# Two-layer hybrid trunk on one Trainium2 core: activation rows split with an adding transfer, wide products one group sooner, runs of three in both layers

## Chip, core and metric

The kernel runs on one core of a Trainium2 chip. The metric is the time of one execution of the whole program on the device in microseconds (us), as the median of several runs. The engines are named as the profile names them: PE is TensorE, which multiplies matrices (PEld is its loading of weights), DVE is VectorE, ACT is ScalarE, POOL is GpSimd, SP is SyncE. SP issues the loads from memory; POOL issues the transfers that add while they copy. All of them are carried by the core's 16 DMA engines.

## The reference

The input is x with 512 tokens of 1024 numbers. Two layers run one after the other. Each has a mixer (layer 0: short convolution and pooling heads; layer 1: spatial gating in chunks) and then a gated feed-forward block with a causal convolution between up-projection and activation. The change is in the feed-forward block of both layers:

```python
def gated_conv_ffn(x, w_gate, w_up, conv_w, conv_b, w_down):   # D_FF = 2816
    g = jnp.einsum('bsd,df->bsf', x, w_gate)
    g = causal_dwconv3(g, conv_w) + conv_b
    up = jnp.einsum('bsd,df->bsf', x, w_up)
    return jnp.einsum('bsf,fd->bsd', jax.nn.silu(g) * up, w_down)
...
        hn = rms_norm(h, norm_ffn[layer])
        h = h + gated_conv_ffn(hn, w_ffn_gate[layer], w_ffn_up[layer], conv_ffn[layer],
                               b_conv_ffn[layer], w_ffn_down[layer])
    return rms_norm(h, final_norm)
```

All numbers are 32-bit floats.

## The kernel before

**Numbers in two parts.** Every operand of a matmul is kept as a high part, rounded to the reduced format that TensorE takes (float32r), and a low part, what the rounding left. A product is three matmuls: high by high, high by low, low by high. To split a tile, `halves` and `split` (L262) let ScalarE write the high part (L265) and VectorE subtract it from the source (L267). The other way, `summed` (L137), lets ScalarE write the negated, rounded source into the low part (L141), lets a transfer issued by POOL add the source to it (L143), and lets ScalarE write the high part after that (L145). Both give the same two parts, since the low part is the source less its rounding.

**The feed-forward block.** Its 2816 columns are 22 tiles of 128, taken two at a time: f = 0, 2, ..., 20. f=0 is multiplied directly. Every other group of two tiles is computed with the Strassen-Winograd form of a 2 x 2 block product: seven products for the gate `g` and seven for the up-projection `u`, fourteen in the order of `todo` in `products`. Each has four row blocks of 128 (kp = 0 to 3), and each row block takes three matmuls of 256 columns (line 705 of `multiply`). A *wide* product joins two of the three: the high part of the weights multiplies the high and the low part of the moving operand side by side, in one matmul of 512 columns, and the low part of the weights follows with one of 256 (line 695). The two halves of the bank then have to be added: where a narrow product is folded with one VectorE add, or one ScalarE copy (L944), a wide one takes one more VectorE add of 256 columns (L932). For `u`'s product 4 this is a copy and an add (L981 and after it).

**Which are wide.** `FIRST_WIDE` gives, for each layer, the first f at which all products of `g` and of `u` are wide; at the first f of `g`, products 2, 5 and 3 of `u` are too. So the first wide group has ten wide products of fourteen, and the later ones fourteen.

**Their order.** `parts_of` lists, for each product, whether the 512-column matmuls or the 256-column ones (`True` in `lows`) come first. Where all are wide, layer 0 alternates: the first product wide then narrow, the second narrow then wide, and so on. Layer 1 puts three products' narrow matmuls in a row and then three products' wide ones.

**What feeds a group.** `prepare(f)` loads four raw weight tiles of 512 KB on SP's queue, forms the sums that the scheme needs (s12, s34) on VectorE and splits them. The second raw tile of `g` and of `u` goes the way of `summed` (wlo_g, wlo_u); from f=4 on so do s12 and s34 of `g` (L887 to L889). A raw buffer is free for the next load when the last reader, the adding transfer among them, is done.

**The rows.** After a group, VectorE and ScalarE convolve, apply silu and multiply by `u`; this gives two activation rows of 128 x 512. `act` (L752) splits a row with `split` into a_hi and a_lo, for which there are four buffers each. `STEPS` sets when a down-projection runs: two groups' rows (four) are multiplied with one half of the output's columns after the next group and with the other half after the one behind that. The rows of the next two groups can be split only as that second half frees the four buffers. Layer 0's last four rows are used by `d_last`; layer 1's last four are not split by `act` but in the block that ends the kernel.

**What sets the order.** The kernel is written for a framework that orders the instructions of each engine when it is built: among those that are ready by its own costs, the one that stands earlier in the program goes first. `behind` adds an order by hand between two instructions of an engine, `inorder` keeps a stretch as it is written. On the chip each engine, POOL's issues among them, then runs its list in that order, and each instruction waits for its semaphores.

Of the kernel before, what the change touches and what calls it, by code (L numbers as in the profile page):

```python
# [9 lines left out]
F32R = mybir.dt.float32r  # L10
BF16 = mybir.dt.bfloat16
AF = mybir.ActivationFunctionType
ALU = mybir.AluOpType
PSUM = bass.MemoryType.PSUM

P = 128
D = 1024
S = 512
# [3 lines left out]
NF = FF // P  # L22
# [9 lines left out]
def tile_trunk(ctx: ExitStack, tc: tile.TileContext, x, norm_mix, norm_ffn, final_norm,  # L32
# [3 lines left out]
    nc = tc.nc  # L36
# [44 lines left out]
    def behind(ins, first):  # L81

        if first is not None:
            tc.add_manual_dep(ins.ins, first.ins.name, mybir.DependencyInfo(
                mybir.DependencyClass.NoSync, mybir.DependencyReason.DATA), reason="order")
# [176 lines left out]
    def split(pool, src, name, scale=1.0, tag="a", bufs=None):  # L262
        hi = pool.tile([P, S], F32R, tag=f"{tag}hi", bufs=bufs, name=f"{name}_hi")
        lo = pool.tile([P, S], F32R, tag=f"{tag}lo", bufs=bufs, name=f"{name}_lo")
        nc.scalar.activation(hi, src, AF.Copy, scale=scale)  # L265
        if isinstance(scale, float):
            nc.vector.tensor_tensor(lo, src, hi.bitcast(F32), ALU.subtract)  # L267
        else:
            nc.vector.scalar_tensor_tensor(lo, src, scale, hi.bitcast(F32),
                                           op0=ALU.mult, op1=ALU.subtract)  # L270
        return hi, lo
# [15 lines left out]
    def padded_tile():  # L287
        turn[0] += 1
        return padded[turn[0] % NPADDED]
# [382 lines left out]
    PAIRS = [k for i in range(NP) for k in (i, i + NP)]  # L672

    FIRST_BY_DMA = 4
    FIRST_WIDE = ({"g": 6, "u": 8}, {"g": 4, "u": 6})

    BANK = {1: "a", 6: "a", 7: "a", 4: "a", 5: "e", 3: "e", 2: "b"}

# [37 lines left out]
    class Ffn:  # L716
# [33 lines left out]
            return s  # L750

        def act(self, ft, s):  # L752
            self.acts[ft] = split(self.ap, s, f"a{self.layer}_{ft}", tag="a", bufs=4)

        def pair_weights(self, order):

# [155 lines left out]
        def products(self, f, stat):  # L912

            layer, ap, n = self.layer, self.ap, f"{self.layer}_{f}"
            banks = {"g": {}, "u": {}}
            kept = ap.tile([P, 3, HALF], F32, tag="kept", bufs=1, name=f"kept{n}")
            pads = [padded_tile() for _ in range(2)]
            lo, hi = slice(2, 2 + HALF), slice(2 + HALF, 2 + S)
            dst = {("g", 1): pads[0][:, lo], ("g", 6): pads[0][:, hi], ("g", 7): pads[1][:, hi],
                   ("g", 4): pads[1][:, lo]}  # L920
            dst.update({("u", product): kept[:, i, :] for i, product in enumerate((1, 6, 7))})
            onto = {2: 1, 7: 7, 3: 6}
            s = {}

            def in_both(key, product):
                first = FIRST_WIDE[layer]
                return f >= first[key] or f == first["g"] and product in (2, 5, 3)

            def add(d, bank, halves):
                ins = None  # L930
                for half in halves:
                    ins = nc.vector.tensor_tensor(d, bank[:, half * HALF : (half + 1) * HALF], d,  # L932
                                                  ALU.add)
                return ins

            def after(key, product, bank):
                halves = range(1 + in_both(key, product))
                if product in onto:
                    ins = add(dst[key, onto[product]], bank, halves)
                    if product == 7:  # L940
                        self.added[key] = ins
                elif (key, product) != ("u", 4):
                    d = dst[key, 7 if product == 5 else product]
                    nc.scalar.copy(d, bank[:, :HALF])  # L944
                    add(d, bank, halves[1:])

            todo = [("g", 1), ("u", 1), ("g", 2), ("g", 5), ("g", 6), ("u", 5), ("u", 6),
                    ("g", 7), ("u", 2), ("u", 7), ("g", 3), ("u", 3), ("g", 4), ("u", 4)]
            if layer and all(in_both(*at) for at in todo):
                parts_of = [(0, (False,))]  # L950
                for i in range(0, len(todo), 3):
                    parts_of += [(j, (True,)) for j in range(i, min(i + 3, len(todo)))]
                    parts_of += [(j, (False,)) for j in range(i + 1, min(i + 4, len(todo)))]
            else:
                parts_of = [(i, (i % 2 == 1, i % 2 == 0)) for i in range(len(todo))]
            begun = set()
            for i, lows in parts_of:
                key, product = todo[i]
                bank = self.multiply(banks[key], f"{key}{n}", product, stat[key, product],
                                     in_both(key, product), lows)  # L960
                if len(lows) == 1 and i not in begun:
                    begun.add(i)
                    continue
                after(key, product, bank)
                if (key, product) in (("g", 4), ("g", 3)):
                    j = product == 4
                    row = pads[j][:, 2:]
                    nc.vector.tensor_tensor(row, row, self.r, ALU.mult)  # L968
                    s[j] = self.silu(self.conv(pads[j], f + j), f + j)
                    if j and layer == 0:  # L970
                        nc.vector.tensor_tensor(s[1], s[1], self.r, ALU.mult)
            if layer == 0:
                nc.vector.tensor_tensor(kept[:, :2, :], kept[:, :2, :],
                                        self.r.rearrange("p (a b) -> p a b", a=2), ALU.mult)
            s0 = s[0].rearrange("p (a b) -> p a b", a=2)
            nc.vector.tensor_tensor(s0, kept[:, :2, :], s0, ALU.mult)
            nc.vector.tensor_tensor(s[1][:, HALF:], kept[:, 2, :], s[1][:, HALF:], ALU.mult)
            last = bank[:, :HALF]
            if in_both("u", 4):
                last = kept[:, 0, :]  # L980
                nc.scalar.copy(last, bank[:, :HALF])  # L981
                add(last, bank, (1,))
            nc.vector.tensor_tensor(s[1][:, :HALF], last, s[1][:, :HALF], ALU.mult)
            return [(f + 1, s[1]), (f, s[0])]
# [358 lines left out]
    def ffn1(norm):  # L1343
        with tc.tile_pool(name="f1", bufs=1) as ap:
# [108 lines left out]
            def product(p, i, c0=0, c1=512, bank=None):  # L1453
# [14 lines left out]
                return ps  # L1468

            vec, act, pool = nc.vector, nc.scalar, nc.gpsimd  # L1470
            rows_f = [wp.tile([P, D], F32, tag="raw", bufs=4, name=f"yf{t}") for t in range(NT)]
            factor, root = ([ssf[:, t, i : i + 1] for t in range(NT)] for i in (4, 5))
# [91 lines left out]
            refined(0, 1)  # L1564
            taken(7, 1, right)
            scaled(act, 0, left)
            scaled(act, 0, right)
            stored(0, slice(0, D))
            all_but_last(2, right)
# [84 lines left out]
```

## Time and profile before

| | us |
|---|---|
| median of 3 runs (lowest, highest) | 966.72 (966.33, 968.95) |
| the profiled execution, its own time | 966.66 |
| its span, first to last instruction | 964.9 |

| engine | busy us | share of the span |
|---|---|---|
| PE | 956.6 | 99% |
| DVE | 847.2 | 88% |
| ACT | 620.8 | 64% |
| POOL | 162.4 | 17% |

The granted clock of TensorE is 0.999 over the span. The feed-forward block of layer 0 stands at about 144 to 460 us of the span, that of layer 1 at about 632 us to the end. In the page's row of the 16 DMA engines' busy share, most slices of these stretches stand at 4 to 8 tenths.

How to read the rows that follow: a group row gives line, engine, operation, out<-in by the program's names (without buffer numbers), partitions x elements and count, then busy time in us and the mean duration in ns, then the idle time of the engine before these instructions and who ended it. A row of the timeline starts with the start and the duration in us; what stands in brackets is the idle time before it. Matmuls overlap, so the distance between two starts, and not a matmul's duration, is what TensorE pays for one.

### The profile page before, as it was taken

The page shows a single profiled execution, that of the slowest core. Times are in us where ns is not written, and L with a number is a line of the kernel's source. Part 1 is how long each engine was busy: PE and PEld are TensorE (multiplying, and loading weights), DVE is VectorE, ACT ScalarE, POOL GpSimd, SP SyncE. Part 2 cuts the span into 40 slices and gives each one's busy share as a digit, 9 for nine tenths or more (in the row PEclk, how much of TensorE's full clock was granted, in tenths as well). Part 3 has the DMA queues.
Part 4 walks back from the last instruction along what each step waited for, and adds up shares of the span by engine and source line. Part 5 has one row for each costly group of instructions (what it writes and reads, how often), then busy time and mean ns, then how long its engine had stood idle before and what let it go on. Part 6 is the DMA issues. An engine that isn't in the chain of part 4 may idle for free.

```text
span 964.9 us, 14240 instructions
## 1 busy us (share of the span) xinstructions
PE 956.6 (99%) x5155; PEld 826.5 (86%) x5155; DVE 847.2 (88%) x1435; ACT 620.8 (64%) x944; POOL 162.4 (17%) x183
## 2 busy tenths in 40 slices
PE   9999999999999999999999999999999999999997
PEld 7888898998888888888888888989888888888885
DVE  6887988989899998998878689889998989989898
ACT  5524667766576565765487847787765566646676
POOL 2142333111011010110311002321111011110124
PEclk9999999999999999999999999999999999999999
DMA  7442345777777578774452323467776777667865
GB/s 253 146 141 87 66 144 120 179 188 178 176 174 176 153 175 197 164 180 137 131 153 88 109 88 88 138 134 184 186 181 175 182 176 174 167 168 177 207 146 152
DMA packets 95538, 150.47 MB, mean 156 GB/s; under 512 B 5252, under 2 KB 61548, under 8 KB 95468
## 3 DMA queue, kind: packets, MB, share of 16 engines
q1 hardware_dynamic: 77996, 98.69, 32.8%
q0 software_dynamic: 15696, 49.03, 27.8%
q10 hardware_dynamic: 1776, 1.84, 0.6%
q8 instruction: 41, 0.67, 0.3%
q14 instruction: 29, 0.24, 0.1%
HBM read 98.42 MB, written 2.10 MB: 104 GB/s over the span
## 4 chain that ended last, share of the span: by engine, by line
PE 99%; DMA 0%; DVE 0%; issue 0%; SPq 0%; ACT 0%; DVEq 0%
PE dn L156 3%; PE d L157 3%; PE d L156 3%; PE dn L157 3%; PE d L158 3%; PE dn L158 3%; PE vu_a L1166 2%; PE gu L156 2%; PE gu L158 2%; PE gu L157 2%; PE u_2a L705 1%; PE g_2a L705 1%; PE u_4a L705 1%; PE g_6a L695 1%; PE u_12a L695 1%; PE u_16a L695 1%
## 5 line engine op out<-in xcount | busy, mean ns | idle before, releaser
L143 POOL DMA_DIRECT2D wlo_g<-raw_g x20 | 17.2, 860 | 318.8 <-ACT wlo_g L141 66.5
L741 DVE SCALAR_TENSOR_TENSOR c<-rows,prm,c 128x512 f32<-128x512 f32 x88 | 64.9, 746 | 1.2 <-ACT c L739 1.0
L156 PE MATMUL d<-a_hi,whi_d 128*128 128x512 f32 x144 | 56.1, 389 | 0.0
L156 PE MATMUL dn<-whi_dn,a_hi 128*128 128x512 f32 x144 | 56.1, 389 | 0.0
L157 PE MATMUL d<-a_lo,whi_d 128*128 128x512 f32 x144 | 56.1, 389 | 0.0
L157 PE MATMUL dn<-wlo_dn,a_hi 128*128 128x512 f32 x144 | 56.0, 389 | 0.0
L158 PE MATMUL d<-a_hi,wlo_d 128*128 128x512 f32 x144 | 56.0, 389 | 0.0
L158 PE MATMUL dn<-whi_dn,a_lo 128*128 128x512 f32 x144 | 56.0, 389 | 0.0
L856 ACT ACTIVATE whi_a<-raw_g 128x512 fp32r<-128x512 f32 x20 | 12.6, 632 | 67.2 <-PE g_18e L695 9.4
L739 ACT ACTIVATE c<-rows,prm 128x512 f32<-128x512 f32 x44 | 31.3, 714 | 10.2 <-DVE rows L968 10.1
L1371 DVE SCALAR_TENSOR_TENSOR y<-dn,small,y 128x512 f32<-128x512 f32 x40 | 28.0, 749 | 6.7 <-PE dn L158 6.7
L749 ACT ACTIVATE s<-c,prm 128x512 f32<-128x512 f32 x44 | 31.4, 715 | 3.2 <-DVE c L741 3.0
L265 ACT ACTIVATE a_hi<-s 128x512 fp32r<-128x512 f32 x40 | 24.7, 626 | 12.2 <-PE d L158 9.4
L201 ACT ACTIVATE hg<-h,prm 128x512 fp32r<-128x512 f32 x24 | 17.2, 719 | 23.5 <-DVE h L314 17.0
L158 PEld LDWEIGHTS dn<-whi_dn,a_lo 128*128 128x128 f32 x144 | 27.0, 188 | 5.7
L158 PEld LDWEIGHTS d<-a_hi,wlo_d 128*128 128x128 f32 x144 | 27.0, 188 | 5.6
L157 PEld LDWEIGHTS dn<-wlo_dn,a_hi 128*128 128x128 f32 x144 | 27.0, 188 | 5.6
L156 PEld LDWEIGHTS d<-a_hi,whi_d 128*128 128x128 f32 x144 | 27.0, 188 | 5.6
L156 PEld LDWEIGHTS dn<-whi_dn,a_hi 128*128 128x128 f32 x144 | 27.0, 188 | 5.6
L157 PEld LDWEIGHTS d<-a_lo,whi_d 128*128 128x128 f32 x144 | 27.0, 188 | 5.5
L141 ACT ACTIVATE wlo_g<-raw_g 128x1024 fp32r<-128x1024 f32 x20 | 21.0, 1048 | 16.3 <-PE g_2e L705 7.6
L152 DVE TENSOR_TENSOR wlo_d<-raw_d,whi_d 128x1024 fp32r<-128x1024 f32 x18 | 22.0, 1224 | 10.4 <-ACT whi_d L151 10.4
(1279 smaller groups left out, 3377.6 us busy)
## 6 DMA issues: line engine op xcount, KB each, us to landing
raw_g<-in_w_ffn_gate_dram SPq DMA_DIRECT2D x40, 512.0 KB, 3.8
raw_u<-in_w_ffn_up_dram SPq DMA_DIRECT2D x40, 512.0 KB, 3.7
raw_dn<-in_w_ffn_down_dram SPq DMA_DIRECT2D x22, 512.0 KB, 3.5
wlo_g<-raw_g POOLq DMA_DIRECT2D x20, 512.0 KB, 5.2
wlo_u<-raw_u POOLq DMA_DIRECT2D x20, 512.0 KB, 6.1
raw_d<-in_w_ffn_down_dram SPq DMA_DIRECT2D x18, 512.0 KB, 4.1
wlo_s12g<-s12g POOLq DMA_DIRECT2D x18, 512.0 KB, 6.6
wlo_s34g<-s34g POOLq DMA_DIRECT2D x18, 512.0 KB, 6.2
```

The costliest lines, as they stand in the source:

```text
L141: first = nc.scalar.activation(lo, raw, AF.Copy, scale=-1.0)
L152: behind(nc.vector.tensor_tensor(lo, raw, hi.bitcast(F32), ALU.subtract), after[0])
L156: nc.tensor.matmul(ps, lhs[0], rhs[0], start=start, stop=False, skip_group_check=skip)
L157: nc.tensor.matmul(ps, lhs[0], rhs[1], start=False, stop=False, skip_group_check=skip)
L158: nc.tensor.matmul(ps, lhs[1], rhs[0], start=False, stop=stop, skip_group_check=skip)
L265: nc.scalar.activation(hi, src, AF.Copy, scale=scale)
L695: last_matmul[0] = nc.tensor.matmul(ps if low else banks[at], left(kp)[low], right(kp)[0] if low else both(kp), start=first, stop=kp == NP ...
L705: nc.tensor.matmul(ps, l, r, start=first, stop=end, skip_group_check=True)
L739: nc.scalar.activation(c, t[:, 0:S], AF.Copy, scale=prm("cf", ft))
L741: self.last_conv = nc.vector.scalar_tensor_tensor(c, t[:, i : S + i], prm("cf", i * NF + ft), c, op0=ALU.mult, op1=ALU.add)
L749: self.last_silu = nc.scalar.activation(s, c, AF.Silu, bias=self.prm("bf", ft))
L1371: return nc.vector.scalar_tensor_tensor(dst, ps, ffn.cols[:, t : t + 1], dst, op0=ALU.mult, op1=ALU.add)
```

## The change

Three edits, all in the feed-forward block:

- `act` no longer calls `split` for the tiles ft = 0 to 17 of either layer. For these, ScalarE writes the negated, rounded row into a_lo, a transfer issued by POOL adds the row to it, and ScalarE writes a_hi behind the first copy. Tiles 18 to 21 are split as before.
- `FIRST_WIDE` is two smaller everywhere. In layer 0, f=4 becomes the first wide group and f=6 is all wide; in layer 1, these are f=2 and f=4.
- Runs of three are used in layer 0 too, except in its last group, f=20.

```diff
-    FIRST_WIDE = ({"g": 6, "u": 8}, {"g": 4, "u": 6})
+    FIRST_WIDE = ({"g": 4, "u": 6}, {"g": 2, "u": 4})
...
         def act(self, ft, s):
-            self.acts[ft] = split(self.ap, s, f"a{self.layer}_{ft}", tag="a", bufs=4)
+            name = f"a{self.layer}_{ft}"
+            if not (ft < NF - 4):
+                self.acts[ft] = split(self.ap, s, name, tag="a", bufs=4)
+                return
+            hi = self.ap.tile([P, S], F32R, tag="ahi", bufs=4, name=f"{name}_hi")
+            lo = self.ap.tile([P, S], F32R, tag="alo", bufs=4, name=f"{name}_lo")
+            first = nc.scalar.activation(lo, s, AF.Copy, scale=-1.0)
+            nc.gpsimd.dma_start(lo, s, accum_op=ALU.add)
+            behind(nc.scalar.activation(hi, s, AF.Copy), first)
+            self.acts[ft] = hi, lo
...
-            if layer and all(in_both(*at) for at in todo):
+            if (layer or f + 2 < NF) and all(in_both(*at) for at in todo):
```

## The prediction

> **What bounds the kernel now.** I read the page's busy times and its chain of what ended last, then who waited for whom on TensorE (PE).
>
> ```profile
> span 964.9 us, 14240 instructions
> PE 956.6 (99%) x5155; PEld 826.5 (86%) x5155; DVE 847.2 (88%) x1435; ACT 620.8 (64%) x944; POOL 162.4 (17%) x183
> PE 99%; DMA 0%; DVE 0%; issue 0%; SPq 0%; ACT 0%; DVEq 0%
> ...
> PE z L417 <- ACT whi_z L410: 0.3, 1, 0.3
> ```
>
> The chain is TensorE from end to end, and the one wait listed for it on another engine's work is 0.3 us, in the first microseconds. So relief of VectorE (DVE) or ScalarE (ACT) buys nothing by itself. Time can only go if TensorE's own instructions take less, and it can only come back as new waits of TensorE. What TensorE pays for a group of two feed-forward tiles (14 products of 4 row blocks) is read from the timeline: the start of a group's first matmul, and of the first matmul after it.
>
> ```profile
> 191.45 0.40 PE L705 MATMUL g_4a<-hg,whi_a 128*128 128x256 f32 x2
> ...
> 211.60 0.40 PE L156 MATMUL d<-a_hi,whi_d 128*128 128x512 f32 x1
> ...
> 217.07 0.39 PE L695 MATMUL g_6a<-hg,whi_a 128*128 128x512 f32 x1
> ...
> 237.10 0.40 PE L156 MATMUL d<-a_hi,whi_d 128*128 128x512 f32 x1
> ...
> 248.00 0.39 PE L695 MATMUL g_8a<-hg,whi_a 128*128 128x512 f32 x1
> ...
> 267.55 0.39 PE L156 MATMUL d<-a_hi,whi_d 128*128 128x512 f32 x1
> ...
> 400.20 0.39 PE L695 MATMUL g_18a<-hg,whi_a 128*128 128x512 f32 x1
> ...
> 419.77 0.39 PE L156 MATMUL d<-a_hi,whi_d 128*128 128x512 f32 x1
> ...
> 644.62 0.40 PE L705 MATMUL g_2a<-hg,whi_a 128*128 128x256 f32 x2
> ...
> 664.77 0.40 PE L156 MATMUL dn<-whi_dn,a_hi 128*128 128x512 f32 x1
> ...
> 670.24 0.39 PE L695 MATMUL g_4a<-hg,whi_a 128*128 128x512 f32 x1
> ...
> 689.93 0.40 PE L156 MATMUL dn<-whi_dn,a_hi 128*128 128x512 f32 x1
> ...
> 695.40 0.39 PE L695 MATMUL g_6a<-hg,whi_a 128*128 128x512 f32 x1
> ...
> 714.92 0.39 PE L156 MATMUL dn<-whi_dn,a_hi 128*128 128x512 f32 x1
> ```
>
> The differences give the price list. Narrow group (all 256 columns): 20.15 us (191.45 to 211.60; the same in layer 1, 644.62 to 664.77). First wide group, where ten of the 14 products are wide: 20.03 in layer 0 (from 217.07), 19.69 in layer 1 (from 670.24). All wide, narrow and wide matmuls alternating: 19.55 (from 248.00) and 19.57 (from 400.20). All wide in runs of three: 19.52 (from 695.40).
>
> **The change part by part.**
>
> *Wide products sooner.* Two narrow matmuls become one of 512 columns: the columns stay the same, and only what each matmul adds goes. Layer 0, f=4: from 20.15 to the first-wide form. Layer 1's 19.69 is that form without a loss; layer 0's 20.03 has the same matmuls and loses 0.34. I credit 20.15 - 19.69 = 0.46 and book the loss apart. Layer 1, f=2: the same 0.46. Layer 0, f=6: 20.03 to all wide in runs, 20.03 - 19.52 = 0.51. Layer 1, f=4: 19.69 - 19.52 = 0.17.
>
> *Runs of three in layer 0.* f=8 to 18, six groups between 19.55 and 19.57; with their mean, 6 x (19.56 - 19.52) = 0.24. f=20 is excepted by the edit.
>
> Sum on TensorE: 0.46 + 0.46 + 0.51 + 0.17 + 0.24 = 1.84 us less.
>
> At this point a rule of the Trainium skill differs. Its page TensorE: Matmul & The Clock Gate, section Back-to-back issue gap, gives an isolated warm matmul N/2.4 + 2.5 ns; by that, as an estimate, 12 narrow matmuls take 1.310 us and 4 wide plus 4 narrow 1.300, so the 28 newly wide products would save 0.3 us. The trace disagrees: 20.15/14 = 1.439 against 19.52/14 = 1.394 us a product. I go by the trace.
>
> *What the wide products add.* Each costs one more add on VectorE to fold the bank's second half (L932), and for u's product 4 a copy on ScalarE too: 10 in each first-wide group, 4 in each group that goes from first-wide to all wide.
>
> *Low parts moved.* 18 rows a layer, 36 in all, lose VectorE's subtraction (L267) and gain a second ScalarE copy, an issue on POOL and a 256 KB adding transfer. The other 4 of the 40 subtractions stay.
>
> ```profile
> L932 DVE TENSOR_TENSOR kept<-u_20a,kept 128x256 f32<-128x256 f32 x10 | 4.2, 422 | 0.8 <-PE u_20a L695 0.8
> ...
> L267 DVE TENSOR_TENSOR a_lo<-s,a_hi 128x512 fp32r<-128x512 f32 x40 | 26.8, 685 | 0.2
> ...
> L265 ACT ACTIVATE a_hi<-s 128x512 fp32r<-128x512 f32 x40 | 24.7, 626 | 12.2 <-PE d L158 9.4 <-PE dn L157 2.3
> ...
> L143 POOL DMA_DIRECT2D wlo_u<-raw_u x20: 859/859/862, 167.4 to 905.2; - x20
> ...
> t<-t POOLq DMA_DIRECT2D x4, 256.0 KB, 3.7
> ...
> q0 software_dynamic: 15696, 49.03, 27.8%
> ```
>
> VectorE: 28 adds x 0.422 = 11.8 us more, 36 x 0.685 = 24.7 less. ScalarE: 36 x 0.626 = 22.5 more, on an engine busy 64%. POOL: 36 x 0.86 = 31 us of issue on an engine busy 17%. Transfers: the adding queue moved 49.03 MB in 27.8% of 964.9 = 268 us, 5.47 us a MB, so a row of 0.262 MB costs all 16 engines 1.43 us. None of this is TensorE's, so it costs nothing as long as the operands come in time. I look at that in three places.
>
> (a) *The rows themselves.* In a full group they are written as the down-projection before it frees their four buffers, and are read at the next one, a group of 19.5 us later; 0.63 + 0.86 + 3.7 us fits. The tightest are rows 0 and 1 in the second group:
>
> ```profile
> L267 DVE TENSOR_TENSOR a_lo<-s,a_hi x2: 684/684/685, 177.5 to 178.1; 128x512 fp32r<-128x512 f32 x2
> ...
> 185.98 0.40 PE L156 MATMUL d<-a_hi,whi_d 128*128 128x512 f32 x1
> ```
>
> The subtractions start at 177.5 and 178.1, the first user at 185.98. If a copy and an issue take that place, the second row, behind the first one's issue, lands at about 178.1 + 0.63 + 0.86 + 3.7 = 183.3: 2.7 us to spare. Cost nothing; it would cost what a transfer takes beyond that.
>
> (b) *VectorE in the first wide groups.*
>
> ```profile
> 191.50:217.10 25.60, 25.60 (x194) 24.64 (x193) 22.34 (x37) 18.07 (x28) 3.44 (x4) 1.00 0.82 197
> ...
> 644.60:670.20 25.60, 25.60 (x193) 24.66 (x192) 23.93 (x40) 20.63 (x31) 3.44 (x4) 1.00 0.66 161
> ...
> 746.00:750.00 4.00, 4.00 (x19) 3.33 (x18) 3.97 (x7) 4.00 (x7) 0.60 (x1) 1.00 1.07 215
> ...
> 754.00:758.00 4.00, 4.00 (x23) 3.46 (x22) 3.64 (x6) 3.21 (x5) 0.86 (x1) 1.00 1.04 208
> 758.00:762.00 4.00, 4.00 (x24) 3.51 (x24) 3.97 (x8) 1.47 (x3) 0.00 (x0) 1.00 0.31 46
> ```
>
> The columns after the stretch and its length are PE, PEld, DVE, ACT, POOL, granted clock, DMA share and GB/s. Two rows' subtractions go in each of the first two stretches and ten adds come: VectorE 22.34 + 4.2 - 1.4 = 25.2 of 25.6 in layer 0, 23.93 + 4.2 - 1.4 = 26.8 of 25.6 in layer 1. It is full, so weight sums and bank reads behind it can be late. Nearest rows for the price: layer 0's present first wide group loses 0.34 us, layer 1's nothing. I take half for each of the two, 0.34 together; the bounds are 0 and 2 x 0.34 plus layer 1's overload of 1.2, 1.9 us.
>
> (c) *The transfers that share POOL and the DMA engines with the rows.* Rows are split where u's low part (wlo_u) and g's s34 are being added. In layer 0's group f=10, and in layer 1's f=6:
>
> ```profile
> 275.92 0.63 ACT L265 ACTIVATE a_hi<-s 128x512 fp32r<-128x512 f32 x1 [2.09 <-PE d L158]
> ...
> 279.30 0.61 ACT L265 ACTIVATE a_hi<-s 128x512 fp32r<-128x512 f32 x1
> ...
> 279.69 0.86 POOL L143 DMA_DIRECT2D wlo_u<-raw_u  x1 [1.04 <-ACT wlo_u L141]
> ...
> DMA to landing us min/median/max: 5.5/5.5/5.5
> ...
> 290.54 0.52 PE L695 MATMUL u_10b<-hg,wlo_u 128*128 128x256 f32 x3
> ...
> 695.06 0.86 POOL L143 DMA_DIRECT2D wlo_u<-raw_u  x1 [2.27 <-ACT wlo_u L141]
> ...
> DMA to landing us min/median/max: 6.7/6.7/6.7
> ...
> 705.63 0.64 PE L695 MATMUL u_6b<-hg,wlo_u 128*128 128x256 f32 x4
> ```
>
> POOL issues in order, so a row whose buffer is not yet free (ScalarE waits for the down-projection at 275.92) holds up what stands behind it: wlo_u, then the raw buffer its landing releases and the next weight load on SP. Before, wlo_u landed at 279.69 + 5.5 = 285.2 for a use at 290.54. Runs of three need it sooner: in layer 1 it is read 705.63 - 695.40 = 10.2 us after the group's start, which in layer 0's f=10 (it starts one down-projection, 248.00 - 237.10 = 10.9 us, after 267.55, at 278.4) is 288.6. Room left: 3.4 us there, 705.63 - 695.06 - 6.7 = 3.9 in layer 1's f=6. The row ahead costs one copy and one issue, 0.63 + 0.86 = 1.5 us, and its transfer 1.43 if the engines are full: 2.9, inside 3.4. So nothing, taken at the near end; the far end is the rival below.
>
> A rule that speaks against this: the skill's page SBUF — State Buffer says that GpSimd and VectorE share a port pair as an exclusive lock, so an adding transfer's descriptors can wait for VectorE (the box on the "DVE blocks DMA" trap). As an estimate, one blocked subtraction of 1.2 us ahead of each of two issues would use up the room. The trace does not show it: 20 issues last 859 to 862 ns beside a VectorE that is 88% busy.
>
> **The sum.** The profiled execution took 966.66 us, 1.76 outside its span, and the median of the runs is 966.72. 966.66 - 1.84 + 0.34 = 965.16, so **965.2 us**.
>
> **The rivals.**
>
> *Late behind the rows (slower).* If POOL's order puts all four rows of a group ahead of wlo_u, or their transfers share full engines with it (DMA share 1.07 and 1.04 in layer 1's stretches around the split), it lands up to 4 x 1.43 = 5.7 us later, or 7.4 with two issues. TensorE then waits 5.7 - 3.4 = 2.3 us in layer 0's f=10, 14, 18 and 1.8 in layer 1's f=6: 8.7 us, 973.5; with 7.4, 15.5 us and 980. It decides from a delay of 3.4 us. For it: full engines just there. Against: the share falls to 0.31 right after (758 to 762), and the rows are spread over the down-projection, 275.92 to 279.30 for the last two, not in one burst.
>
> *VectorE becomes the bound in the first wide groups.* Far end of (b): 966.66 - 1.84 + 1.9 = 966.7, no change. For it: 26.8 of 25.6. Against: the subtractions that leave later let it catch up within a group.
>
> *A stall undone elsewhere (faster).* To be 0.3% faster (2.9 us; about what a measurement of this kernel tells from no change) some 1.1 us beyond 1.84 would have to go, and the 0.3 of waits above is all there is to give back.
>
> *The move frees nothing that matters.* Part of the forecast: the 12.9 us net that VectorE loses appear nowhere in the span.
>
> **How the numbers follow.** Forecast 0.58, with 964.8 to 966.0 as its own range (1.84 in full; or the loss of (b) at twice what I take and 0.5 of (c)); VectorE bound 0.19; late behind the rows 0.18, most of it above 969.6; faster 0.05. Within 0.3% come the first two and a slight form of the third: faster 0.05, same 0.78, slower 0.17. The range leaves out the longer part of the slower rival, and starts at the full 1.84 less the 0.39 by which the lowest run shown (966.33) lies under the median: 964.4 to 970.0.
>
> **What would show it.** Right: groups f=4 and f=2 near 19.7, later ones near 19.52 in both layers; a_lo off VectorE but for 4; no TensorE wait in the chain. Wrong: TensorE waiting in f=10, 14, 18 on wlo_u, with POOL showing row transfers ahead of it; a first wide group over 20.15; a down-projection waiting on a row's transfer.

## The result and the profile after

| | median us (lowest to highest, runs) | ratio [95%] |
|---|---|---|
| before | 966.82 (966.33 to 968.95, 6) | |
| after | 976.98 (974.49 to 979.76, 6) | 1.0103 [1.0093, 1.0113] |

The change costs 1%. The forecast was 965.2, between 964.4 and 970.0: the time went the other way, and out of the range. First the page of after (span, busy times, what the chain of what ended last consists of, the queue of adding transfers), then who TensorE waited for.

```profile
span 976.1 us, 14164 instructions
PE 959.3 (98%) x5043; PEld 822.4 (84%) x5043; DVE 836.4 (86%) x1427; ACT 637.5 (65%) x982; POOL 193.6 (20%) x219
PE 88%; DMA 5%; issue 3%; DVE 2%; ACT 1%; POOL 1%; DVEq 0%; SPq 0%; POOLq 0%; ACTq 0%
...
q0 software_dynamic: 20880, 58.47, 33.5%
```
```profile
PE u_8b L695 <- DMA wlo_u<-raw_u: 2.4, 2, 1.2
PE u_4b L695 <- DMA wlo_u<-raw_u: 1.9, 1, 1.9
PE u_4e L695 <- DVE wlo_s12u L866: 1.5, 1, 1.5
PE u_10b L695 <- DMA wlo_u<-raw_u: 1.3, 1, 1.3
PE z L417 <- ACT whi_z L410: 1.1, 1, 1.1
...
PE g_4a L695 <- DMA wlo_s34g<-s34g: 0.6, 1, 0.6
```

VectorE did lose 10.8 us (847.2 to 836.4), and the chain, 99% TensorE before, now passes through DMA, VectorE, ScalarE and POOL: 9% of it stands there, and 3% at "issue", time in which an engine waited for nothing that the profile shows. In the feed-forward blocks TensorE's waits are for *low parts of weights* (wlo_u, wlo_s12u, wlo_s34g), but for one of 0.2 us for a fold in f=10. No wait is for a row's a_lo. The timeline of TensorE says which groups pay, again by the start of a group's first matmul and of the first one after it:

```profile
192.25 0.39 PE L695 MATMUL g_4a<-hg,whi_a 128*128 128x512 f32 x1
...
212.17 0.40 PE L156 MATMUL d<-a_hi,whi_d 128*128 128x512 f32 x1
...
217.64 0.39 PE L695 MATMUL g_6a<-hg,whi_a 128*128 128x512 f32 x1
...
237.45 0.39 PE L156 MATMUL d<-a_hi,whi_d 128*128 128x512 f32 x1
...
248.33 0.39 PE L695 MATMUL g_8a<-hg,whi_a 128*128 128x512 f32 x1
...
269.23 0.39 PE L156 MATMUL d<-a_hi,whi_d 128*128 128x512 f32 x1
...
646.09 0.39 PE L695 MATMUL g_2a<-hg,whi_a 128*128 128x512 f32 x1
...
665.89 0.40 PE L156 MATMUL dn<-whi_dn,a_hi 128*128 128x512 f32 x1
...
671.36 0.39 PE L695 MATMUL g_4a<-hg,whi_a 128*128 128x512 f32 x1
...
697.16 0.39 PE L156 MATMUL dn<-whi_dn,a_hi 128*128 128x512 f32 x1
```

Read the same way in every kernel of this study, the groups took (us, from starts before rounding, so the last digit can be off by one from the rows above; the changed kernel's later groups are at 19.51 to 19.55). Each line is one profiled execution; those of e7 and of e11 below took 1.3 and 1.6 us more than the median of their runs.

| kernel | span | L0 f=4 | f=6 | f=8 | L1 f=2 | f=4 | f=6 | f=8 | f=10 |
|---|---|---|---|---|---|---|---|---|---|
| before | 964.9 | 20.15 | 20.03 | 19.55 | 20.15 | 19.70 | 19.52 | 19.51 | 19.51 |
| after | 976.1 | 19.93 | 19.81 | 20.90 | 19.80 | **25.80** | 19.53 | 20.98 | 21.79 |
| e7, no adds | 967.0 | 20.09 | 23.40 | 19.51 | 19.70 | 19.51 | 19.52 | 19.51 | 19.51 |
| e9, sums first | 968.5 | 19.89 | 20.40 | 20.72 | 19.80 | 19.51 | 21.04 | 20.73 | 19.51 |
| e14, both remedies | 963.6 | 19.88 | 19.52 | 19.51 | 19.79 | 19.51 | 20.16 | 19.51 | 19.51 |

From before to after the groups changed by -0.22 - 0.22 + 1.35 in layer 0's f=4 to 8, five times -0.05 in f=10 to 18, and -0.35 + 6.10 + 0.01 + 1.47 + 2.28 in layer 1's f=2 to 10: +10.2 of the span's 11.2 us. Another 0.8 lies ahead of the changed code (layer 0's f=2 starts at 166.63 instead of 165.83; such starts lay between 165.37 and 166.63 in the runs of this study).

**Why layer 1's f=4 is late.** VectorE's timeline in after, from group 2's last folds into the next down-projection:

```profile
662.35 0.68 DVE L886 TENSOR_TENSOR s12g<-raw_g,raw_g 128x512 f32<-128x512 f32 x1
...
663.61 0.68 DVE L977 TENSOR_TENSOR rows<-rows,rstd_f 128x512 f32<-128x512 f32 x1
...
665.14 0.75 DVE L741 SCALAR_TENSOR_TENSOR c<-rows,prm,c 128x512 f32<-128x512 f32 x1
...
667.41 0.68 DVE L907 TENSOR_TENSOR s34g<-raw_g 128x512 f32<-128x512 f32 x1
...
670.85 1.41 DVE L1380 SCALAR_TENSOR_TENSOR y<-dn,small,y 128x512 f32<-128x512 f32 x2
...
673.49 0.69 DVE L909 TENSOR_TENSOR s34g<-raw_g,s12g 128x512 f32<-128x512 f32 x1
674.09 0.69 DVE L886 TENSOR_TENSOR s12u<-raw_u,raw_u 128x512 f32<-128x512 f32 x1
```

The weight sums of group 4 (L886 to L909) stand late in the program, so the order built from it gives them only the gaps between group 2's folds, convolution and gating and the output's adds (L1380). Ten more folds leave no gap: six us lie between the two halves of one sum, 667.41 and 673.49. In the kernel before, whose group 4 began 1.1 us sooner, the same two instructions (L898, L900) started at 658.8 and 659.8, as its view of this tile says; behind it, POOL's timeline in before and then in after:

```profile
L898 DVE TENSOR_TENSOR s34g<-raw_g x2: 683/684/684, 658.8 to 685.3; 128x512 f32<-128x512 f32 x2
L900 DVE TENSOR_TENSOR s34g<-raw_g,s12g x1: 683/683/683, 659.8 to 659.8; 128x512 f32<-128x512 f32 x1
```
```profile
668.49 0.86 POOL L888 DMA_DIRECT2D wlo_s34g<-s34g  x1 [4.19 <-PE dn L158]
670.99 0.86 POOL L143 DMA_DIRECT2D wlo_u<-raw_u  x1 [1.65 <-ACT wlo_u L141]
```
```profile
676.13 0.86 POOL L897 DMA_DIRECT2D wlo_s34g<-s34g  x1
678.02 0.86 POOL L143 DMA_DIRECT2D wlo_u<-raw_u  x1 [1.03 <-ACT wlo_u L141]
```

The sum is 13.7 us late. About 6 us of that was room: ScalarE's copy of it came 6.7 us after the sum in before, at 667.15, and 0.6 us after it in after, at 674.78. The rest goes on to POOL's issue: wlo_s34g is 7.6 us late, and so by 7.0 is wlo_u, which needs no sum but stands behind wlo_s34g in the lists of ScalarE and POOL. wlo_u took 8.1 us to land, at about 686.1, and u_4b began at 686.17 after a wait of 1.9.

Later raw loads wait for the same sums (SP waited for s34g for 12.7 us at the longest, 5.7 in before), and groups 8 and 10 are late in their turn. In f=10 the rows take part. POOL's timeline there:

```profile
764.22 0.86 POOL L897 DMA_DIRECT2D wlo_s34g<-s34g  x1 [0.60 <-ACT wlo_s34g L896]
764.76 1.21 POOL L760 DMA_DIRECT2D a_lo<-s  x1
767.15 0.86 POOL L143 DMA_DIRECT2D wlo_u<-raw_u  x1 [1.19 <-ACT wlo_u L141]
```

This wlo_u took 9.6 us to land, 6.1 in before. The group is late only with the rows' transfers (21.79, and 21.68 in e6 below; 19.51 in e1 and e3, which have none), but with them too it is back at 19.51 once group 4's sums come first (e9, e14). How the 2.3 us divide between late sums and rows is not shown.

### The profile page after: what moved, and what is told of

Same layout as the page of the kernel before. It is cut to its first block, busy times and chain, and to the rows that moved or that the text cites. A ratio compares the mean times of both kernels' runs of the same rounds, so it can differ in the third digit from the quotient of the medians.

```text
span 976.1 us, 14164 instructions
## 1 busy us (share of the span) xinstructions
PE 959.3 (98%) x5043; PEld 822.4 (84%) x5043; DVE 836.4 (86%) x1427; ACT 637.5 (65%) x982; POOL 193.6 (20%) x219
## 3 DMA queue, kind: packets, MB, share of 16 engines
q10 hardware_dynamic: 1776, 1.84, 0.6%
## 4 chain that ended last, share of the span: by engine, by line
PE 88%; DMA 5%; issue 3%; DVE 2%; ACT 1%; POOL 1%; DVEq 0%; SPq 0%; POOLq 0%; ACTq 0%
PE dn L156 3%; PE dn L157 3%; PE dn L158 3%; DMA wlo_u<-raw_u 3%; PE d L156 3%; PE d L157 3%; PE d L158 3%; PE vu_a L1175 2%; DMA raw_g<-in_w_ffn_gate_dram 2%; PE gu L156 2%; PE gu L158 1%; PE gu L157 1%; PE u_20a L695 1%; PE g_18a L695 1%; PE u_16a L695 1%
## 5 line engine op out<-in xcount | busy, mean ns | idle before, releaser
L865 ACT ACTIVATE whi_a<-raw_g 128x512 fp32r<-128x512 f32 x20 | 12.7, 633 | 75.4 <-PE g_8e L695 13.2
L760 POOL DMA_DIRECT2D a_lo<-s x36 | 32.8, 911 | 57.6 <-ACT a_lo L759 47.8
L212 POOL TENSOR_TENSOR ssq_m<-ssq_m,sq_m 128x512 f32<-128x512 f32 x14 | 19.7, 1405 | 65.9 <-ACT sq_m L211 65.9
L1380 DVE SCALAR_TENSOR_TENSOR y<-dn,small,y 128x512 f32<-128x512 f32 x40 | 28.0, 747 | 4.9 <-PE dn L158 4.9
L866 DVE TENSOR_TENSOR wlo_s12u<-s12u,whi_s12u 128x1024 fp32r<-128x1024 f32 x20 | 24.4, 1219 | 7.0 <-ACT whi_s12u L865 7.0
```

Source lines behind the costliest of these rows:

```text
L212: nc.gpsimd.tensor_tensor(self.ssq, self.ssq, sq, ALU.add)
L760: nc.gpsimd.dma_start(lo, s, accum_op=ALU.add)
L1380: return nc.vector.scalar_tensor_tensor(dst, ps, ffn.cols[:, t : t + 1], dst, op0=ALU.mult, op1=ALU.add)
```

## The experiments

Two theories at the start. ADD: the adds that the wide products bring keep VectorE from the sums of the next group's weights. ROW: the rows' transfers and ScalarE's copies delay what shares POOL, ScalarE and the DMA engines with them.

**Each part alone.** e1 is before with the new `FIRST_WIDE` alone, e2 with the new `act` alone, e3 and e4 add the runs of three to e1 and e2.

> Only the wide products one group sooner, in both layers; rows split by VectorE as before, layer 0 alternating. Theory ADD (the extra adds in the first wide groups fill VectorE, so that the weight sums and all that hangs on them come late for several groups): the same late groups as in the changed kernel, layer 1's f=4 over 22 us and f=8 and f=10 over 20.5, time 970 to 976. Theory ROW (ScalarE's and POOL's lists have the rows ahead of the weights, and four more transfers fill the DMA engines): no late group, 0.46 + 0.46 + 0.5 + 0.17 us less and 0.3 lost, so 965.5.

> Only the rows' low parts by ScalarE and an adding transfer; products and their order as before. Theory ROW: most of the 10 us are here, 972 to 978, with TensorE waiting for wlo_u or s34 in layer 1's f=4, f=8 and f=10. Theory ADD: VectorE has 24.7 us less to do and nothing is late: 966.5 to 967.5.

> Wide products sooner and runs of three in layer 0, rows split by VectorE. Theory ADD: as e1, 970 to 976, no better than the changed kernel by more than 2 us, since VectorE has 24.7 us more to do than there. Theory ROW: 0.24 us under e1, about 965.2, the forecast without its loss.

> Rows by the adding transfer and runs of three in layer 0, wide products where they were. Theory ROW: as slow as e2, or slower, since runs of three read wlo_u about 1.9 us sooner after a group's start: 972 to 978. Theory ADD: 966.5, runs of three being worth 0.24. Each alone harmless and only both together late (the two share the room): e1 to e4 all under 968.

| | median us | ratio [95%] |
|---|---|---|
| e1 | 981.43 | 1.0153 [1.0137, 1.0168] |
| e2 | 968.98 | 1.0031 [1.0019, 1.0042] |
| e3 | 982.66 | 1.0164 [1.0147, 1.0181] |
| e4 | 968.42 | 1.0021 [1.0012, 1.0031] |

The wide products alone cost more than the whole change; the new rows win 4 to 6 us of it back (976.98 against 981.43 and 982.66), while by themselves they cost 2 us. In e1 layer 1's f=4 took 24.98 us and f=6 26.62, with no row transfer in the program: the rows are not the cause of the large loss. It was larger than ADD expected (970 to 976 for e1 and e3), and in e1 f=6 was late with f=4, not f=8 and f=10 (20.49 and 19.51). e2 and e4 lie between what the two theories said. In e2 one group alone is late, layer 0's f=6 with 21.94, by one wait:

```profile
PE g_6a L695 <- DVE rows L941: 2.0, 1, 2.0
```

**One layer alone.** The change, with the other layer's `FIRST_WIDE` left as it was.

> The changed kernel with the wide products one group sooner in layer 0 alone (layer 1: 4 and 6 as before). Theory ADD: the room is short where VectorE is overfull, layer 1's f=2 by 26.8 of 25.6 us against layer 0's f=4 by 25.2 of 25.6, so nearly all of the loss goes: 966.0 to 968.5, with no late group in layer 1. If layer 0's share is as large as layer 1's: 971 to 973.

> The changed kernel with the wide products one group sooner in layer 1 alone (layer 0: 6 and 8 as before). Theory ADD: layer 1's f=4, f=8 and f=10 are late as in the changed kernel, 975 to 978.

e5: 968.63, ratio 1.0017 [1.0008, 1.0026]; e6: 979.47, ratio 1.0137 [1.0122, 1.0152], with 27.52 us in layer 1's f=4. Nearly all of the loss belongs to layer 1, whose groups from f=4 on are at 19.5 to 19.7 in e5. The times are 0.1 and 1.5 us above the ranges, and the parts do not add up: e6 is slower than the whole change. e5 keeps 21.42 and 21.28 us in layer 0's f=6 and f=8.

**The adds.** e7 is the change without the second-half adds of the 28 newly wide products, so the second half of these banks is left out of its output; with them goes one ScalarE copy in each layer, for `u`'s product 4. e8 is before, its products narrow as they were, with those 28 adds and two copies put in, each add taking a first half once more.

In e7 `folded` is `in_both` by the old `FIRST_WIDE`; in e8 `twice` names the products that only the new one makes wide.

```diff
-                halves = range(1 + in_both(key, product))
+                halves = range(1 + folded(key, product))
```
```diff
-                halves = range(1 + in_both(key, product))
+                halves = (0,) * (2 if twice(key, product) else 1) if not in_both(key, product) else (0, 1)
```

> The changed kernel without the adds of the second bank half for the 28 newly wide products (that part of their sums is left out, and product 4 of u is multiplied straight from its bank); the matmuls are all there. Theory ADD: no late group, the matmuls' 1.84 us less are kept: 964.5 to 966.5. If the sooner and shorter matmuls or the rows' transfers make the weights late: still above 973.

> The kernel before with the 28 adds alone: in the groups that the change makes wide, the products stay narrow, and their bank half is added a second time (product 4 of u is copied and added to itself). The rows stay with VectorE. Theory ADD: as slow as e1 and slower by the 1.6 us that its matmuls save: 977 to 984. If wide matmuls are needed for the loss: under 969.

e7: 967.46, ratio 1.0008 [0.9999, 1.0017], every group of layer 1 from f=4 on at 19.5 and f=2 at 19.70. e8: 978.72, ratio 1.0129 [1.0112, 1.0146], with 29.60 us in layer 1's f=6:

```profile
PE g_6e L695 <- DMA wlo_s12g<-s12g: 4.0, 1, 4.0
PE g_6e L695 <- ACT whi_s12g L889: 2.8, 1, 2.8
```

Adds of 11.8 us in all cost 12 us with no other edit, again at a weight sum's parts. So ADD, though e7 came out 1.0 us above its range and e8 2.7 us below e1 and not above it. What e7 still loses is layer 0's f=6 (23.40), late as in e2: without that 3.9 us its span would be 963.1, 1.8 below before. Of this 0.4 lies in a feed-forward block that began sooner; the groups give about 1.5, since layer 0's f=4 kept 20.09.

**Order or amount?** e9 is the change with, in layer 1, group 2's row scaling (L977, the first step of its convolution) put behind group 4's gate sums on VectorE. The work is the same.

```diff
+    SUMS_FIRST = ((1, 4),)
...
-                nc.vector.tensor_tensor(s34[:, 1], r1[:, :, :P], s12[:, 1], ALU.subtract)
+                last = nc.vector.tensor_tensor(s34[:, 1], r1[:, :, :P], s12[:, 1], ALU.subtract)
+                if key == "g" and (layer, f) in SUMS_FIRST:
+                    for ins in self.scaled:
+                        behind(ins, last)
...
-                    nc.vector.tensor_tensor(row, row, self.r, ALU.mult)
+                    self.scaled.append(nc.vector.tensor_tensor(row, row, self.r, ALU.mult))
```

> The changed kernel with one thing moved: in layer 1, the row scaling that opens the convolution of group 2 (two instructions of VectorE, one for each row) stands behind the sums of weight blocks for the gate's products of group 4. VectorE does the same instructions in all, in another order. Theory ORDER (the adds of layer 1's group 2 don't cost by their sum, but because the folds, the convolution and the gating of group 2 stand ahead of group 4's weight sums in VectorE's order, so that these start 8 to 13 us late, and with them the adding transfers that end in wlo_s12u and wlo_u): group 4 of layer 1 falls from 25.8 us to between 19.5 and 21.5, and the time to 968 to 972. Theory AMOUNT (VectorE has more to do in groups 2 and 4 than TensorE's time for them covers, whatever the order): what the sums win the convolution loses; the late work appears in group 6 or 8, and the time stays between 975 and 979.

969.77, ratio 1.0033 [1.0022, 1.0045], and layer 1's f=4 at 19.51: two instructions moved win 7.2 us. VectorE's timeline has the sums together now and the convolution behind them:

```profile
664.32 0.68 DVE L909 TENSOR_TENSOR s34g<-raw_g 128x512 f32<-128x512 f32 x1
664.92 0.69 DVE L911 TENSOR_TENSOR s34g<-raw_g,s12g 128x512 f32<-128x512 f32 x1
665.52 0.69 DVE L984 TENSOR_TENSOR rows<-rows,rstd_f 128x512 f32<-128x512 f32 x1
...
668.26 0.75 DVE L743 SCALAR_TENSOR_TENSOR c<-rows,prm,c 128x512 f32<-128x512 f32 x1
```

The busy times of these two groups' stretches, for after and then for e9 (columns as in the prediction), say that VectorE had the time for this work:

```profile
646.10:671.40 25.30, 25.30 (x154) 22.60 (x153) 23.87 (x43) 18.93 (x30) 4.30 (x5) 1.00 0.70 150
671.40:697.00 25.60, 21.66 (x113) 18.21 (x112) 18.42 (x37) 14.06 (x23) 4.30 (x5) 0.93 0.74 179
```
```profile
646.10:671.40 25.30, 25.30 (x154) 22.60 (x153) 23.74 (x44) 20.47 (x32) 5.12 (x6) 1.00 0.73 166
671.40:697.00 25.60, 25.60 (x141) 22.25 (x140) 24.71 (x47) 19.75 (x32) 5.41 (x7) 1.00 0.93 213
```

In after VectorE idled 7.2 of the second 25.6 us, the very group whose time grew; in e9 it did the work within the two groups. Some lateness did move on as AMOUNT said, 1.5 us of it to f=6 (19.53 to 21.04); e14 below, with more of the sums first, brings f=6 to 20.16. The move shifts other lists as well: in e9 POOL issues the next two rows behind wlo_u, in after ahead of it and of wlo_s34g. There wlo_s34g was issued within 0.3 us of ScalarE's copy all the same, and its landing took 7.3 us in both, that of wlo_u 8.1 in after and 7.3 in e9, so that place cost about 1 us by these figures.

**Wide later, and the rows' 2 us.** e10 is before with the runs of three and, in layer 1, `{"g": 4, "u": 4}`. e11 and e13 are e4 with two of layer 0's rows left to `split`, rows 4 and 5 or rows 2 and 3. e12 is e11 with `{"g": 4, "u": 4}`. The edit of e11, which has (2, 3) in e13:

```diff
-            if not (ft < NF - 4):
+            if not (ft < NF - 4) or (self.layer == 0 and ft in (4, 5)):
```

> The kernel before with two parts alone: runs of three in layer 0's groups 8 to 18, and in layer 1 the up products wide from group 4 on, as the gate's are (group 2 stays narrow in all but three, rows stay with VectorE). Four adds of 512 columns come into group 4 of layer 1 where the change brought ten into group 2 and four into group 4. If the price of the adds hangs on how many fall ahead of the weight sums (theory ADD, by its order): group 4 of layer 1 falls from 19.69 to 19.5, layer 0's groups 8 to 18 to 19.51, and the time is 966.2 to 966.5, 0.4 less than before at most. If any add more in the first wide group delays the weights of the next: group 6 of layer 1 takes over 21 us and the time is 968 to 970.

> The kernel before with the low parts of the rows by ScalarE and the adding transfer, except rows 4 and 5 of layer 0, which VectorE keeps, and with the runs of three in layer 0; the wide products stay one group later. The rows and the runs together took 968.42, with 21.34 us in layer 0's group 6. If that group's 1.4 us come from ScalarE's four row copies of group 4's activations ahead of the copy of a bank: group 6 is back between 19.9 and 20.3 and the time is 966.4 to 967.1. If they come from the transfers on the queue or from the wider tiles' buffers, group 6 stays above 21 and the time at 968.

> The last one with the up products of layer 1 wide from group 4 on as well. The transfer takes 4 instructions a pair of rows from VectorE, so if VectorE's room ahead of the weight sums sets the price, the four adds cost nothing here even where they do with VectorE's rows: 0.1 to 0.2 us below the run without them, 966.2 to 967.0. If the adds delay layer 1's group 6 whatever the rows do, 968 or more.

> The kernel before with the low parts of the rows by ScalarE and the adding transfer, except rows 2 and 3 of layer 0, which VectorE keeps, and with the runs of three in layer 0; wide products one group later, as before. With rows 4 and 5 left out instead, layer 0's group 6 took 23.63 us. Theory LOAD (the two row transfers issued at 195 and 197 us share the DMA engines with wlo_u of group 4 and with the raw loads of group 6; the raw up block that ScalarE's narrow copy needs lands 1 to 3 us late, and VectorE's order from there on is as much late at the bank of g_6a): the wait for raw_u is gone, group 6 of layer 0 is between 19.7 and 20.3 and the time is 966.3 to 967.2. Theory COPIES (ScalarE's own row copies of group 4's activations ahead of the copy of a bank): group 6 stays above 21 and the time at 968.

| | median us | ratio [95%] | L0 f=6 | L1 f=4, f=6 |
|---|---|---|---|---|
| e10 | 967.97 | 1.0011 [1.0002, 1.0020] | 19.75 | 19.51, 19.92 |
| e11 | 968.57 | 1.0023 [1.0014, 1.0032] | 23.63 | 19.70, 19.64 |
| e12 | 968.97 | 1.0024 [1.0014, 1.0035] | 21.43 | 19.51, 19.79 |
| e13 | 966.21 | 0.9998 [0.9989, 1.0007] | 19.71 | 19.70, 19.51 |

e10 missed its 966.5. Hardly by its four adds, which won 0.19 in layer 1's f=4 and gave back 0.41 in f=6: layer 0's f=14 and f=18 took 20.26 and 20.15 us, each with a wait of 0.3 us for VectorE's fold of a bank. Runs of three want these folds sooner. In the kernels that have the runs and move the rows off VectorE, all groups from f=10 to 18 stand at 19.51. e12's adds won 0.19 and gave back 0.15; its time lies 2 us above the range for that, with layer 0's f=6 at 21.43.

e11 missed as well, and that tells where the 2 us come from: leaving out the copies that I suspected did not help, leaving out rows 2 and 3 (e13, 0.1 us under its range) did, with no wait left in the block. (The copies for rows 2 and 3, which go with them, are not it: ahead of group 6's narrow copies ScalarE waits 1.0 us for TensorE's u_4a in e11 and in e13.) Of e11, the view of ScalarE's narrow copy whi_a with the wait ahead of it, and the landing of wlo_u of group 4, issued 12 us sooner (5.4 us in before); then the same two views of e13:

```profile
L865 ACT ACTIVATE whi_a<-raw_u x1: 632/632/632, 204.8 to 204.8; 128x512 fp32r<-128x512 f32 x1
...
DMA raw_u<-in_w_ffn_up_dram: 2.6, 1
```
```profile
DMA to landing us min/median/max: 7.4/7.4/7.4
```
```profile
L865 ACT ACTIVATE whi_a<-raw_u x1: 636/636/636, 202.6 to 202.6; 128x512 fp32r<-128x512 f32 x1
```
```profile
DMA to landing us min/median/max: 5.7/5.7/5.7
```

In e11 the two row transfers are issued at 195.40 and 196.70, onto the wlo_u transfer issued at 192.71. That one lands 2 us later, SP waits for it with its next raw loads (3.8 us; 1.3 in before, 1.6 in e13), raw_u comes 2.2 us later to ScalarE, VectorE's list moves with it, and the bank of g_6a is folded late.

That is e11's path, and not the only one. In e2, e4, e6 and e12 wlo_u landed after 5.6 to 5.9 us, as in e13, and group 6 was late all the same. ScalarE's wait for raw_u was 2.8, 1.7, 0.2 and 0.9 us there, f=6 took 21.94, 21.34, 21.55 and 21.43; in e6, whose layer 0 has e4's instructions in e4's order on VectorE, ScalarE, POOL and SP, VectorE waited for raw_g instead, 2.1 us. What they share is where VectorE's first sum for group 6 (s12g) starts, counted from group 4's first matmul: 14.7 to 15.5 us in these four and in e11, 13.2 in e13 and 13.3 in before. So with the transfers of rows 2 and 3 a raw load of group 6 comes late, one time raw_u and another time raw_g. That these transfers slow it by sharing the DMA engines is likely, but no run here separates it.

**Both remedies.** e14 is the change with the sums first ahead of more groups and rows 2 and 3 of layer 0 left to `split`.

```diff
+    SUMS_FIRST = ((0, 6), (0, 8), (1, 4), (1, 6), (1, 8))
...
+            if not (ft < NF - 4) or (self.layer == 0 and ft in (2, 3)):
```

> The changed kernel with both remedies: the row scaling behind the gate's weight sums ahead of groups 6 and 8 of layer 0 and groups 4, 6 and 8 of layer 1 (the run before had it ahead of group 4 of layer 1 alone), and rows 2 and 3 of layer 0 with VectorE. That run's late groups were 6 and 8 of layer 0 (20.40, 20.72) and of layer 1 (21.04, 20.73), 5 us above 19.5 in all. If the order of VectorE's list is what makes them late: all four are between 19.5 and 20.2, and the time is 964.9 to 967.0, as fast as the kernel before or faster. If the transfer that ends in wlo_u is late by its own queue (raw loads, ScalarE's copies), groups 8 keep 20.7 and the time is 967.5 to 969.5.

965.50 us (965.22 to 965.93, 11 runs), ratio 0.9988 [0.9979, 0.9997]: the fastest of this study, 1.2 us below the 966.67 of before, though within the 0.3% that counts as no change here. (In the profiled execution the groups account for 1.0 us; another 0.5 lies ahead of the changed code.) What is left of TensorE's waits in the feed-forward blocks:

```profile
PE u_6e L696 <- DVE wlo_s12u L868: 0.4, 1, 0.4
```

## Why the prediction was wrong, step by step

- **Step (b) failed.** "VectorE in the first wide groups" was priced at 0.34 us, at most 1.9. The place was right, layer 1's first wide group, and so was "weight sums and bank reads behind it can be late"; but the price falls on the groups behind it, 9.9 us in layer 1's f=4, 8 and 10 and 1.35 in layer 0's f=8 (12 us for the adds alone, e8), while f=2 itself took 19.80. I worked it out as a balance, 26.8 us of work in 25.6, and let the excess of 1.2 be the far end. In after VectorE was busy for 23.87 us of that stretch: the sums had slid into the next one. e9 shows that the balance was not the limit: with the same work and another order f=4 takes 19.51 instead of 25.80. What counts is *which* instructions the ten adds push back. They push back the weight sums, which stand late in the program and so get the gaps, and behind these hang three more steps (copy, transfer, use), a load, and the groups after it. The sentence against this rival, that fewer subtractions let VectorE catch up within a group, is half true: the rows' move did win 4 to 6 us (after against e1 and e3).
- **The saving on TensorE was right, term by term.** It was put at 1.84. No run shows all of it at once (e7's groups give 1.5), but each form is found within 0.02 us of its forecast in some run: layer 0's f=4 at 19.69 (e1), its f=6 at 19.52 (e14) and its runs at 19.51, layer 1's f=2 at 19.70 (e7) and f=4 at 19.51. The Trainium skill's figure for an isolated matmul in TensorE: Matmul & The Clock Gate, Back-to-back issue gap, weighed there at 0.3 us, does not give this saving.
- **Step (c) failed, at 2 us (e2), and in another group than the one looked at.** "Nothing" was argued from the room ahead of wlo_u in the full groups, f=10 on, and in layer 0 and in layer 1's f=6 it held. Step (c) named the raw buffer and the next load behind wlo_u, but not the narrow groups ahead, where a raw tile is wanted as soon as it lands. In the changed kernel this cost differs from one execution to the next: layer 0's f=6 took 19.81 in after, but 20.40 in e9 and 21.42 in e5, where VectorE, ScalarE, POOL and SP have the same instructions in the same order from group 4 to group 6.
- **Late behind the rows**, the slower rival, named f=10, 14 and 18 of layer 0 and f=6 of layer 1: no wait there. What it describes is seen in layer 1's f=10 alone, 1.3 us of wait. That its time, 973.5 to 980, holds the result is luck: e1 and e3, without any row transfer, are slower still. The Trainium skill's box on the "DVE blocks DMA" trap in SBUF — State Buffer is not seen in the issues: the 36 of rows lasted 0.86 us in the median and 1.21 at most. Whether the longer landings owe something to it, no run here shows.
- **Step (a) held.** No down-projection waited for a row, though 256 KB took 7.4 us in the median to land and not 3.7. The tightest, layer 0's rows 0 and 1, landed after at most 5.9.
- **Runs of three** cost no more than said where the rows are off VectorE; with VectorE's rows they lose 1.4 us in two groups (e10). And "the move frees nothing that matters" fell: the move is what pays for the runs and for part of the wide products.

## What to carry to other kernels

Before an engine that is 88% busy is given more work, read what only gets the *gaps* in its order and what hangs on that: a balance of busy time over a stretch bounds the cost only if the engine may do its work in any order. When a stage gains work, put the next stage's preparation ahead of this stage's finish by hand and run that too; here two ordering edges were worth 7 us. A new transfer is to be looked up against every load that is consumed the moment it lands, in the stages that differ from the steady one first.

## What the runs showed of the hardware

A wait of TensorE can cost more than its length, and not always. In after, the waits in layer 1's f=4 add up to 4.0 us, but the group lost 6.3; right behind them the granted clock (the column behind POOL) fell, and matmuls of 512 columns that started 0.23 us apart stood about 0.43 apart:

```profile
684.00:688.00 4.00, 2.14 (x12) 1.70 (x11) 1.76 (x4) 1.17 (x3) 0.00 (x0) 0.95 0.83 209
688.00:692.00 4.00, 4.00 (x16) 3.28 (x16) 2.20 (x6) 0.21 (x1) 0.00 (x0) 0.62 0.75 253
692.00:696.00 4.00, 4.00 (x25) 3.51 (x25) 3.59 (x9) 1.12 (x2) 0.86 (x1) 1.00 0.26 50
```

A single wait of 1.8 us did it in e11, and one of 2.0 in e2 did not, at the same place of the program; the stretch right after it in the one and in the other:

```profile
224.00:228.00 4.00, 2.70 (x10) 2.33 (x11) 3.47 (x7) 2.14 (x3) 0.00 (x0) 0.74 0.69 164
```
```profile
224.00:228.00 4.00, 3.44 (x21) 3.09 (x22) 3.84 (x7) 3.18 (x7) 0.43 (x1) 1.00 1.02 191
```

So layer 0's f=6 took 23.63 in e11 and 21.94 in e2. e7 went as e11: a wait of 1.8 us, clock 0.76 and 0.81 in the two stretches from 224 on, 23.40. What decides whether the clock falls stays open.
